# A decoder layer on one core: the first query block's products for the first half of the tokens moved between the two halves of keys and values, a tile of 32 extra rows, and five bridging products

## The chip, the core and the metric

The kernel runs on one core of a Trainium2 chip. The metric is the device time of one execution, in microseconds (us); the kernel before took 1930.22 to 1931.68 us in three runs, median 1931.51 us. A core has several engines, each with a queue of its own that it works through in order: TensorE (PE in the profile; its weight loads are the row PEld), VectorE (DVE), ScalarE (ACT), GpSimd (POOL) and SyncE (SP), which here only issues DMA transfers. An engine waits at the head of its queue until what its next instruction needs is there, and everything behind that instruction waits too. TensorE's clock is granted by the chip and shown in the profile as a share of full speed.

## The reference: what is computed

One step of a hybrid decoder layer for 512 prompt tokens, 16 learned meta tokens ahead of them and 8 single sample tokens, all in fp32, width 2048.

```python
hp = layer_norm(concat([meta, x_prompt]))      # 16 + 512 rows of 2048
hs = layer_norm(x_sample)                      # 8 rows
z = h @ w_in + b_in                            # columns: q 1024 | k 256 | v 256 | u 1024
q, k = partial_rope(q, pos), partial_rope(k, pos)
a = sink_attention(q, k, v, window=128)        # 16 heads of 64, 4 key/value heads, per-head sinks
p = pool_mixer(u)                              # trailing means over 2/4/8/16 positions, linear map, scale
h1 = layer_norm(ALPHA * h + concat([a, p]) @ w_o)
y = layer_norm(ALPHA * h1 + (silu(h1 @ w_gate) * (h1 @ w_up)) @ w_down)
```

The outputs are the new hidden rows of prompt and sample tokens, and the new windows of keys, values and pooling inputs.

## The kernel before

**Tokens and columns.** All activations are held transposed: features on the 128 partitions, tokens along the columns. There are 536 columns: 16 meta, 8 sample, 512 prompt. They are worked on in two halves: the first of 276 columns (0 to 275), the second of 260. Sixteen tiles of 128 features make up the width of 2048.

**A product in fp32.** Weights and activations are split into a high part, made by a cast to a shorter format, and the residual. Each product is three matmuls: high weight by high activation (L203), high by low (L204), low by high (L206). `split` casts a piece of weights, 128 x 512, on ScalarE (L187) and takes the residual on VectorE (L188). The two parts lie in a ring of places, `wh` and `wl`: seven places (WK) up to the end of keys and values, and after that a new ring of four (WA) laid over the room of the first. A cast into a place waits until the matmuls that read that place are done. The raw weights come by SyncE's DMA queue, 512 KB at a time, into a ring of five places (NRAW), and each such load waits for its place in that ring.

**The front.** The 536 token rows come in as four blocks of 128 rows (`xt`, each in four pieces of 512 columns) and one tile `xe` of the extra rows that do not fill a block: 32 rows around the end of the first half and 32 at the end of the second. `xe` is loaded first on SyncE; block 1 is loaded on ScalarE's own DMA queue, block 0 on SyncE's. Meanwhile TensorE multiplies constants 52 times (NWARM, L301); the result is not used. VectorE takes the statistics of the blocks (L310), ScalarE those of `xe` (L325 to L330). `normalisers` works out scale and shift, `x_norm` normalises (L341 on ScalarE; the extra rows on VectorE), `x_turn` transposes 128 x 128 pieces on TensorE into PSUM (L366), and `x_split` applies the gain and bias of the norm (L372 on VectorE, L375 on ScalarE), splits the result (cast L378 on ScalarE, residual L379 on VectorE) and writes it to memory on SyncE's queue.

**Keys and values** are the first products, the four column blocks 0 to 3 of `w_in`. They are made for the first half of the tokens, all sixteen feature tiles, and then for the second. In the loops, `kv_mm(h, k2)` is the step with the 24 matmuls for two feature tiles of half h, accumulating in four PSUM banks (`kv`), and the transposes, splits, and weight splits (`kv_weights`) for a later step stand between two such steps. Each key/value weight is loaded and split once per half. Between the last steps of the first half stand the first normalising and the first transposes of the second half's rows. After each half four instructions write the accumulators out with their bias, two on ScalarE (L477) and two on VectorE (L474).

**After that** come, in this order, query block 0 (`q_block(0)`: `in_block` makes the 96 products of both halves under each split piece of weights, four pieces for each of the two loads), pooling block 0, rotation of keys and their transposes, and then attention, further query and pooling blocks, the output projection, and the feed-forward part with its two norms.

**What sets the order.** The program is written as a list of steps, and a scheduler lays each engine's instructions into its queue by readiness and priority. In the front, `step(engines)` forces the order: on the engines named, every instruction of one step stands behind those of the step before. Inside a step, and after the front, the scheduler chooses. From query block 0 on, weight loads and splits have a raised priority (`prio[0] = WPRIO`). The places in the rings `wh`, `wl` and `raw` are handed out in the order of the program, one after the other.

Of the kernel before, what the change touches and what calls it, by code (L numbers as in the profile page):

```python
# [44 lines left out]
NWARM = 52  # L45
# [10 lines left out]
NB0 = C_P + P  # L56
SWAP = [i + 8 if i < 8 else i - 8 if i < 16 else i for i in range(32)]
# [10 lines left out]
def hybrid_step(ctx, tc, xin, w_in, w_o, w_g, w_u, w_d, w_pool, par_d, cst_d, ident_d, ln2gb, kct_d, vc_d, hist_d,  # L68
# [186 lines left out]
    with ExitStack() as sa:  # L255
# [32 lines left out]
        nc.sync.dma_start(xe[0:32], xin[256:288, :])  # L288
        nc.sync.dma_start(xe[32:64], xin[C_ALL - 32:C_ALL, :])
        nc.gpsimd.memset(xe[64:P], 0.0)  # L290
# [25 lines left out]
        def stats_e():  # L316

            t = pa.tile([P, 2, 2, 256], F32, tag="s", name="sq_e", bufs=2).rearrange("p a b c -> p (a b c)")[:64]
            ac = pa.tile([P, 2, 2], F32, name="ac")[:64]
            nm = pa.tile([P, 1], F32, name="nm_e")[:64]  # L320
            for i in range(2):
                for c in range(2):
                    x = xe[:64, c * 1024:(c + 1) * 1024]
                    if i == 0:
                        nc.scalar.activation(t, x, AF.Identity, accum_out=ac[:, i, c:c + 1])  # L325
                    else:
                        nc.scalar.activation(t, x, AF.Square, bias=nm, accum_out=ac[:, i, c:c + 1])
                nc.scalar.activation(t[:, 0:2], ac[:, i], AF.Identity, scale=1.0 / D, accum_out=mv[0][:64, 2, i:i + 1])
                if i == 0:
                    nc.scalar.activation(nm, mv[0][:64, 2, 0:1], AF.Copy, scale=-1.0)  # L330
# [20 lines left out]
        def x_norm(h, c):  # L351
            for i in range(2):
                norm[h](xt[2 * h + i][c], i, nc.scalar)
            if h == 0:
                norm[h](xe[:64, c * 512:(c + 1) * 512], 2, nc.vector)

        def x_turn(h, c):
            n = xw[h]
            for kk in range(4):
# [4 lines left out]
                for i in (0, 1, 2) if h == 0 else (2, 0, 1):  # L364
                    x, o = (xe[:, c * 512:(c + 1) * 512], 256 - 60 * h) if i == 2 else (xt[2 * h + i][c], i * P)
# [55 lines left out]

        three = (nc.tensor, nc.vector, nc.scalar)
# [13 lines left out]
        out = kv_banks(0)  # L436
        with step(*three):
            x_split(0, 0)
        with step(*three):
            kv_weights(0, range(4))  # L440
        for h in range(2):
            for g in range(4):
                n = h * 4 + g + 1
                with step(*three):
# [26 lines left out]
            with step(*three):  # L471
                for i in range(4):
                    if i % 2:
                        nc.vector.tensor_scalar(zkv[i][:, XH[h]], out[i], par[:, PBIAS + i:PBIAS + i + 1], None,  # L474
                                                op0=ALU.add)
                    else:
# [1045 lines left out]
```

## Time and profile before

| what | value |
|---|---|
| three runs | 1930.22, 1931.51, 1931.68 us; median 1931.51 |
| the profiled execution's own time (its span, first to last instruction) | 1931.1 us |
| mean granted clock of TensorE in it | 0.992 |
| instructions | 39334 |
| key/value matmuls (L203, L204, L206; 128 each in the records) | 32.4, 36.7 and 35.8 us busy |
| transposes of the front (L366; 64 and 32) | 9.8 and 6.3 us busy |
| normalising on ScalarE (L341, 16) | 12.1 us busy |
| HBM traffic | 265.22 MB read, 54.03 MB written |

The span is measured by the profiler inside the device; it lies 0.4 us under the median of the runs. A row of the page's groups gives source line, engine, operation, result and operands by the program's names (buffer numbers left out), shapes, count, busy time, mean length in ns, and then the time that the engine was idle just before these instructions, with what ended it ("<-"). Names: `rr` is the room of split weights and activations, `fr` and `mid_a` are rooms of fp32 tiles, `kv`, `xt`, `mm_q`, `mm_u` are PSUM tiles. A list of single instructions gives start and length in us from the span's start, engine, line and what it is, with the idle time ahead of it in brackets. In the table of windows each row is a stretch of the execution. A matmul with fp32 operands that are not split, such as the constant products and the transposes, can take two passes, and each pass is a record.

### The profile page before, as it was taken

Reading aid. Unit: us, or ns where it says so; the run is one execution under the profiler, and the core shown is the slowest. Engines: PE = TensorE matmul, PEld = TensorE weight load, DVE = VectorE, ACT = ScalarE, POOL = GpSimd, SP = SyncE. Lnnn points to the kernel's source line nnn. Section 1 sums busy time; section 2 is a strip of 40 time slices with the busy share of each in tenths; the row PEclk is TensorE's granted clock in tenths of the full one; section 3 lists DMA queues with packets and bytes.
Section 4 is the critical chain, followed back from the end, with each engine's and each line's share of the span. In section 5 each row is a group of like instructions: output and inputs, shape, how many; then the busy total and the mean of one; then the engine's idle time right before and its main releaser. Section 6 shows DMA issues by size and latency. Waiting matters only on the chain.

```text
span 1931.1 us, 39334 instructions
## 1 busy us (share of the span) xinstructions
PE 1894.4 (98%) x15533; PEld 1865.8 (97%) x15533; DVE 1539.9 (80%) x2734; ACT 944.1 (49%) x1808; POOL 2.7 (0%) x9
## 2 busy tenths in 40 slices
PE   9999999999999999999999999999999999999996
PEld 8999999999989999999999999999999999999996
DVE  6666667768777888888888888888877888888878
ACT  6644445545654544554455555555554444344341
POOL 0000000000000000000000000000000000000000
PEclk9999999999999999999999999999999999999998
DMA  8732222665744555454545445454469664645332
GB/s 276 233 101 66 71 78 75 211 202 193 250 150 164 160 160 172 142 162 158 175 139 178 141 138 165 146 167 145 164 212 356 214 221 162 223 163 202 94 99 89
DMA packets 145241, 319.28 MB, mean 165 GB/s; under 512 B 14288, under 2 KB 66232, under 8 KB 144952
## 3 DMA queue, kind: packets, MB, share of 16 engines
q1 hardware_dynamic: 144480, 315.71, 49.7%
q8 instruction: 122, 2.00, 0.4%
q10 hardware_dynamic: 576, 1.05, 0.2%
q14 instruction: 63, 0.52, 0.1%
HBM read 265.22 MB, written 54.03 MB: 165 GB/s over the span
## 4 chain that ended last, share of the span: by engine, by line
PE 92%; DVE 4%; ACT 2%; DMA 1%; issue 1%; SPq 0%; DVEq 0%; ACTq 0%
PE p_g L203 7%; PE p_g L204 7%; PE p_g L206 7%; PE p_u L203 7%; PE p_u L206 7%; PE p_u L204 7%; PE tri L203 7%; PE tri L206 7%; PE tri L204 7%; PE o L203 3%; PE o L206 3%; PE o L204 3%; PE p_u L996 2%; PE mm_u L203 2%; PE mm_u L206 2%; PE mm_u L204 2%
## 5 line engine op out<-in xcount | busy, mean ns | idle before, releaser
L187 ACT CAST rr<-fr 128x512 fp32r<-128x512 f32 (+1 forms) x1056 | 658.0, 643 | 776.6 <-DVE fr L196 224.0
L188 DVE TENSOR_TENSOR rr<-fr,rr 128x512 fp32r<-128x512 f32 (+1 forms) x1056 | 738.0, 717 | 264.5 <-ACT rr L187 253.2
L196 DVE TENSOR_TENSOR fr<-fr 128x1024 f32<-128x1024 f32 (+1 forms) x304 | 319.7, 1052 | 5.8 <-DMA fr<-in_w_g_dram 5.0
L203 PE MATMUL p_g<-rr 128*128 128x260 f32 x830 | 235.5, 285 | 7.4 <-ACT rr L187 7.1
L206 PE MATMUL p_g<-rr 128*128 128x260 f32 x830 | 230.6, 282 | 0.0
L204 PE MATMUL p_g<-rr 128*128 128x260 f32 x788 | 221.8, 282 | 0.0
L203 PE MATMUL p_u<-rr 128*128 128x260 f32 x770 | 217.5, 283 | 0.2 <-ACT rr L187 0.2
L206 PE MATMUL p_u<-rr 128*128 128x260 f32 x770 | 215.3, 282 | 0.0
L204 PE MATMUL p_u<-rr 128*128 128x260 f32 x748 | 210.6, 282 | 0.0
L206 PE MATMUL tri<-rr 128*128 128x260 f32 x696 | 196.8, 283 | 1.5 <-DVE rr L188 1.5
L203 PE MATMUL tri<-rr 128*128 128x260 f32 x696 | 197.0, 283 | 0.7 <-ACT rr L187 0.7
L204 PE MATMUL tri<-rr 128*128 128x260 f32 x696 | 196.7, 283 | 0.0
L203 PEld LDWEIGHTS p_g<-rr 128*128 128x128 f32 x830 | 156.2, 188 | 9.9 <-ACT rr L187 9.4
L206 PEld LDWEIGHTS p_g<-rr 128*128 128x128 f32 x830 | 155.2, 189 | 0.0
L204 PEld LDWEIGHTS p_g<-rr 128*128 128x128 f32 x788 | 148.1, 188 | 0.0
L203 PE MATMUL o<-rr 128*128 128x260 f32 x512 | 145.0, 284 | 0.3 <-ACT rr L187 0.3
L203 PEld LDWEIGHTS p_u<-rr 128*128 128x128 f32 x770 | 144.9, 188 | 0.3 <-ACT rr L187 0.3
L206 PEld LDWEIGHTS p_u<-rr 128*128 128x128 f32 x770 | 144.6, 189 | 0.0
L204 PE MATMUL o<-rr 128*128 128x260 f32 x512 | 144.1, 282 | 0.0
L206 PE MATMUL o<-rr 128*128 128x260 f32 x512 | 143.6, 282 | 0.2 <-DVE rr L188 0.2
L204 PEld LDWEIGHTS p_u<-rr 128*128 128x128 f32 x748 | 140.6, 188 | 0.0
L206 PEld LDWEIGHTS tri<-rr 128*128 128x128 f32 x696 | 131.3, 189 | 2.2 <-DVE rr L188 2.2
(320 smaller groups left out, 4570.0 us busy)
## 6 DMA issues: line engine op xcount, KB each, us to landing
fr<-in_w_u_dram SPq DMA_DIRECT2D x100, 512.0 KB
fr<-in_w_g_dram SPq DMA_DIRECT2D x90, 512.0 KB
fr<-in_w_d_dram SPq DMA_DIRECT2D x64, 640.0 KB
t_d<-fr SPq DMA_DIRECT2D x140, 260.0 KB
fr<-in_w_o_dram SPq DMA_DIRECT2D x64, 512.0 KB
fr<-in_w_in_dram SPq DMA_DIRECT2D x48, 512.0 KB
rr<-t_d SPq DMA_DIRECT2D x87, 260.0 KB
mid_b<-t_d SPq DMA_DIRECT2D x53, 260.0 KB
```

Of the source, the lines that this page charges most:

```text
L187: nc.scalar.copy(wh, s)
L188: last_lo[0] = (lo or nc.vector).tensor_sub(wl, s, wh.bitcast(F32)).ins
L196: i = op(*args).ins
L203: nc.tensor.matmul(o, wh, hi[j], start=first, stop=False, skip_group_check=onto)
L204: nc.tensor.matmul(o, wh, lo[j], start=False, stop=False, skip_group_check=onto)
L206: nc.tensor.matmul(o, wl, hi[j], start=False, stop=last, skip_group_check=onto)
L996: nc.tensor.matmul(bk, self.q(0, n - 1)[:, k * P:(k + 1) * P], z1[0][4 * (n - 1) + k // 2][:, k % 2, :], start=(k == 0), stop=(k == 7))
```

## The change

Four things are changed, all in the front and in query block 0.

1. **The tile of extra rows** has 32 rows (NE) where it had 64: 20 rows at the end of the first half (256 to 275), and the 12 last rows. Its loads, statistics, normalising and the offsets of its transposes follow.
2. **Warm-up and bridge.** NWARM is 50 where it was 52, and five further products of constants (NBRIDGE, L448) stand between the first transposes, `x_turn(0, 0)`, and the first `x_split` and key/value products. They write into a bank that the key/value products overwrite later.
3. **Query block 0, first half of the tokens.** Its 48 products (3 matmuls for each of 16 feature tiles) are made between the two halves of keys and values, in the generator `q0_half`: four chunks of twelve, each behind the split of its piece of weights. The order there is written out by hand for n = 4: chunk 1 in the step of `kv_mm(0, 6)`, chunk 2 in that of `kv_mm(0, 7)`, then three of the four groups of transposes of the second half's first rows, chunks 3 and 4, and the weight splits for the second half's first step. `load_kvw(1)` moves behind chunk 4.
4. **Query block 0, second half of the tokens** is made where the whole block was made before. Its weights are loaded and split there as before, so that they are now loaded and split twice. Its result `zq0` lies in the ring `q`, and the rotation is done in place.

All line numbers of the changed kernel are higher than before by 2 in the front and by more further on: L205, L206 and L208 are the three matmuls, L189 the cast and L190 the residual of a weight split, L279 a load of `xt`, L328 the first statistic of `xe`, L369 the transposes.

In the rows of order below, each row is one or more equal instructions in an engine's queue, with what they write and read. The first place is on TensorE, at the end of the first half of keys and values: `kv_0` are the first half's accumulators, `xt_0` the second half's transposes, `q_0` the moved query products. Before, and then in the change:

```order
L206 MATMUL kv_0_198<-rr 128x276
L203 MATMUL kv_0_198<-rr 128x276
L204 MATMUL kv_0_198<-rr 128x276
L206 MATMUL kv_0_198<-rr 128x276
L366 MATMUL xt_00_522<-fr,mid_a 128x128
L366 MATMUL xt_01_526<-fr,mid_a 128x128
```

```order
L205 MATMUL kv_0_197<-rr 128x276
L206 MATMUL kv_0_197<-rr 128x276
L208 MATMUL kv_0_197<-rr 128x276
L205 MATMUL q_0_526<-rr 128x260
L206 MATMUL q_0_526<-rr 128x260
L208 MATMUL q_0_526<-rr 128x260
```

The second half's transposes stood directly behind the key/value step `kv_mm(0, 6)`; now the first chunk of query products stands there, and the transposes come later.

The second place is on ScalarE, in the change, ahead of that first chunk: L239 is the square root of the second half's normaliser, L344 its normalising, L378 and L381 the last step of the first half's activation split, L189 x2 casts of query weights.

```order
L239 ACTIVATE mid_a<-mid_a 128x2
L344 ACTIVATE fr<-fr,mid_a 128x512 x2
L378 ACTIVATE fr<-xt_33_441,fr 128x276
L381 CAST rr<-fr 128x552
L189 CAST rr<-fr 128x512 x2
```

The casts of the query weights are new at this place, and they stand behind the normalising of the second half's rows.

The third place is on VectorE, at the end of the second half of keys and values and the start of the query products that follow. L474 and L427 write keys and values out, L395 and L398 rotate them, L188 and L190 are residuals of weight splits, L704 belongs to pooling. Before, and then in the change:

```order
L379 TENSOR_TENSOR rr<-fr,rr 128x520
L474 TENSOR_SCALAR mid_a<-kv_1_582,fr 128x260
L188 TENSOR_TENSOR rr<-fr,rr 128x512
L395 STREAM_SHUFFLE fr<-mid_a 128x536
L395 STREAM_SHUFFLE mid_a<-mid_a 128x536
```

```order
L190 TENSOR_TENSOR rr<-fr,rr 128x512
L427 TENSOR_SCALAR mid_a<-kv_1_617,fr 128x260
L398 STREAM_SHUFFLE mid_a<-mid_a 128x536
L190 TENSOR_TENSOR rr<-fr,rr 128x512 x2
L427 TENSOR_SCALAR mid_a<-kv_1_619,fr 128x260
L398 STREAM_SHUFFLE fr<-mid_a 128x536
L704 TENSOR_REDUCE mid_a<-fr 128x8
L190 TENSOR_TENSOR rr<-fr,rr 128x512
```

Before, the first residual of the query block (L188) stood behind the first write-out. In the change the residual that belongs to the first piece of the second query half is the last row shown; the three L190 rows above it belong to pieces two to four.

The diff, cut to its core:

```diff
-NWARM = 52
+NWARM = 50
+NBRIDGE = 5
...
+NE = 32
...
-        nc.sync.dma_start(xe[0:32], xin[256:288, :])
-        nc.sync.dma_start(xe[32:64], xin[C_ALL - 32:C_ALL, :])
-        nc.gpsimd.memset(xe[64:P], 0.0)
+        nc.sync.dma_start(xe[0:XN - 256], xin[256:XN, :])
+        nc.sync.dma_start(xe[XN - 256:NE], xin[C_ALL - NE + XN - 256:C_ALL, :])
+        for a, b in ((NE, 64), (64, P)):
+            nc.gpsimd.memset(xe[a:b], 0.0)
         load_x(1, nc.scalar)
         load_x(0)
...
-                    x = xe[:64, c * 1024:(c + 1) * 1024]
+                    x = xe[:NE, c * 1024:(c + 1) * 1024]
...
-        def x_turn(h, c):
+        def x_turn(h, c, kks=range(4)):
             n = xw[h]
-            for kk in range(4):
+            for kk in kks:
...
-                    x, o = (xe[:, c * 512:(c + 1) * 512], 256 - 60 * h) if i == 2 else (xt[2 * h + i][c], i * P)
+                    x, o = (xe[:, c * 512:(c + 1) * 512], 256 - (NE - 4) * h) if i == 2 else (xt[2 * h + i][c], i * P)
...
+        def zkv_out(h, i):
+            if i % 2:
+                nc.vector.tensor_scalar(zkv[i][:, XH[h]], out[i], par[:, PBIAS + i:PBIAS + i + 1], None, op0=ALU.add)
+            else:
+                nc.scalar.activation(zkv[i][:, XH[h]], out[i], AF.Identity, bias=par[:, PBIAS + i:PBIAS + i + 1])
...
         out = kv_banks(0)
+        with step(nc.tensor):
+            for j in range(NBRIDGE):
+                nc.tensor.matmul(out[3][:, 0:P], onesd, onesd, start=True, stop=True)
         with step(*three):
             x_split(0, 0)
         with step(*three):
             kv_weights(0, range(4))
+        zq0 = pa.tile([P, C_ALL], F32, tag="q", name="q0", bufs=3)
+
+        def q0_half(h):
+
+            cs, co = ((slice(META, XN), slice(META, XN)), (slice(0, xw[1]), XH[1]))[h]
+            o = (aux_tile([P, 512], "o", "q0_0", 1) if h == 0 else mm_tile("mm_q0_1"))[:, :cs.stop - cs.start]
+            for x in range(2):
+                raw = load_raw(w_in[4][:, x * 1024:(x + 1) * 1024], f"q0_{h}{x}")
+                for g in range(2):
+                    w = split(raw[:, g * 512:(g + 1) * 512], f"q0_{h}{x}{g}")
+                    for kk in range(4):
+                        k, sl = 8 * x + 4 * g + kk, slice(kk * P, (kk + 1) * P)
+                        products([o], w[0][:, sl], w[1][:, sl], [xhi[h][:, k, cs]], [xlo[h][:, k, cs]], k == 0, k == KT - 1)
+                    yield
+            nc.vector.tensor_scalar(zq0[:, co], o, par[:, PBIAS + 4:PBIAS + 5], 0.125, op0=ALU.add, op1=ALU.mult)
+            yield
+
         for h in range(2):
             for g in range(4):
                 n = h * 4 + g + 1
+                if n == 4:
+                    with step(*three):
+                        x_split(0, 7)
+                    for k2 in (6, 7):
+                        with step(*three):
+                            kv_mm(0, k2)
+                            if k2 == 6:
+                                q0 = q0_half(0)
+                                next(q0)
+                            else:
+                                next(q0)
+                                for i in range(4):
+                                    zkv_out(0, i)
+                    with step(*three):
+                        x_turn(1, 0, range(3))
+                    with step(*three):
+                        next(q0)
+                        x_split(1, 0)
+                    out = kv_banks(1)
+                    kvw.pop(0, None)
+                    with step(*three):
+                        next(q0)
+                        kv_weights(0, range(2))
+                    load_kvw(1)
+                    with step(*three):
+                        next(q0)
+                        x_turn(1, 0, [3])
+                        kv_weights(0, range(2, 4))
+                    continue
                 with step(*three):
                     x_split(h, 2 * g + 1)
...
-            with step(*three):
-                for i in range(4):
...
-                if h == 0:
-                    out = kv_banks(1)
+        with step(*three):
+            for i in range(4):
+                zkv_out(1, i)
...
         def q_block(t):
-            out = in_block(4 + t, f"q{t}", META)
-            z = zt_tile(f"zq{t}")
...
+            if t:
+                out = in_block(4 + t, f"q{t}", META)
+                z = zt_tile(f"zq{t}")
...
+            else:
+                for _ in q0_half(1):
+                    pass
+                z = q = zq0
             rope(z, q, f"q{t}", META)
```

25 lines of the change are left out of this document (10 added, 15 removed).

## The prediction

> **What bounds the kernel now.** I read the page's first parts, then the stretches of the clock, then who TensorE waited for, then the chain of waits and the order of time around each wait.
>
> ```profile
> span 1931.1 us, 39334 instructions
> PE 1894.4 (98%) x15533; PEld 1865.8 (97%) x15533; DVE 1539.9 (80%) x2734; ACT 944.1 (49%) x1808; POOL 2.7 (0%) x9
> PE 92%; DVE 4%; ACT 2%; DMA 1%; issue 1%; SPq 0%; DVEq 0%; ACTq 0%
> ```
>
> TensorE sets the time. It is busy for 98% of the span and makes 92% of the chain, so a microsecond won or lost on it in the first 110 us is carried to the end. The stretches below give, for each, its length and the busy time of PE, PEld, DVE, ACT and POOL, then the granted clock, the DMA share and GB/s.
>
> ```profile
> 0.00:14.40 14.40, 13.27 (x104) 13.08 (x104) 6.24 (x15) 7.27 (x16) 2.46 (x8) 1.00 0.87 275
> 14.40:17.80 3.40, 1.76 (x12) 1.31 (x12) 1.51 (x5) 1.96 (x3) 0.00 (x0) 0.97 1.05 390
> 17.80:21.20 3.40, 2.21 (x10) 2.00 (x9) 2.54 (x5) 3.37 (x8) 0.00 (x0) 0.50 1.05 385
> 21.20:24.60 3.40, 3.40 (x18) 3.40 (x16) 2.95 (x6) 3.40 (x6) 0.00 (x0) 0.53 1.09 356
> 24.60:48.50 23.90, 23.43 (x185) 22.62 (x183) 19.62 (x38) 13.80 (x25) 0.00 (x0) 1.00 0.75 233
> 48.50:51.90 3.40, 2.09 (x11) 1.31 (x12) 1.07 (x5) 2.94 (x5) 0.00 (x0) 0.97 0.16 60
> 51.90:55.30 3.40, 3.40 (x16) 3.40 (x17) 2.74 (x5) 2.31 (x6) 0.00 (x0) 0.52 0.38 123
> 55.30:82.50 27.20, 27.20 (x232) 27.16 (x231) 17.82 (x32) 19.99 (x38) 0.00 (x0) 1.00 0.80 231
> 82.50:110.00 27.50, 27.17 (x226) 26.65 (x227) 17.84 (x38) 10.32 (x23) 0.00 (x0) 1.00 0.64 233
> ```
>
> Two things are lost in the front: holes in TensorE's work, and the half clock behind each. A stretch of 3.4 us in which it was busy for 1.76 us (52%) is followed by 6.8 us near 0.50; one with 2.09 us (61%) by 3.4 us at 0.52; after 2.21 us (65%) the half clock stays. Each such stretch, filled, costs half its length: 1.7 us. From 55.3 to 110 only 0.33 us is idle.
>
> **The change, part by part.** All sums are against the profiled span of 1931.1 us; the median of the runs, 1931.51, lies 0.4 above it, and I add the sum to the median.
>
> *Smaller tile of extra rows, 50 warm-up products.* Fewer bytes come first, but the fourth piece of the second token block, whose issue stood ahead of the statistics on ScalarE's queue, now stands behind the first statistic, which waits for the extra rows.
>
> ```profile
> 7.18 1.06 ACT L325 ACTIVATE mid_a<-mid_a 64x1024 f32<-64x1024 f32 x1 [4.01 <-DMA mid_a<-in_xin_dram]
> 9.04 3.22 DVE L310 BATCH_NORM_STATS2 mid_a<-fr 128x6 f32<-128x512 f32 x5 [0.82 <-DMA fr<-in_xin_dram]
> ```
>
> At 390 GB/s 256 KB are 0.7 us, at 275 1.0 us: the gain, at most. The moved piece, two places later, lands some 1.4 us later than in turn, and VectorE needs it sixth of eight; the loss is at most that. I take 0, with −1.0 and +1.3 as ends. ScalarE's casts get no cheaper by fewer rows, since a row of a tile is a partition.
>
> *Five bridging products.* They stand between the first transposes and the first key/value products.
>
> ```profile
> 0.99 13.27 PE L301 MATMUL wb<-fr 128*128 128x128 f32 x104 [0.99 <-POOL fr L143]
> 15.89 0.55 PE L366 MATMUL xt<-fr 128*128 128x128 f32 x3 [1.63 <-ACT fr L341]
> 19.20 0.60 PE L203 MATMUL kv<-rr 128*128 128x276 f32 x1 [1.19 <-ACT rr L187]
> ```
>
> Each product is two passes (104 for 52), 128 ns on average. Two fewer warm-ups widen the 1.63 us hole by 0.5 us, so the stretch ahead stays low and the half clock still comes. Ten passes at half clock are 10 x 0.26 = 2.6 us against a hole of 1.2: they hold the first products up by some 1.0 us. But the stretch is then full, and the clock rises one stretch (3.4 us) sooner: −1.7. Net −0.8. If the clock never falls, the 5.4 us of half clock from 19.2 to 24.6 give −2.7; if it rises no sooner, the delay is left, +1.0.
>
> *Query products into the hole between the halves.* The first instructions behind the last but one key/value step were transposes; now they are twelve query products, and the transposes have gone behind these (TensorE's rows of order, shown with the change). On ScalarE, by its rows there, the query cast (L189) stands behind the very work that made the hole. Before, it went so (TensorE's rows, then the chain of waits with start, length and what):
>
> ```profile
> 47.86 0.38 PE L366 MATMUL xt<-fr,mid_a 128*128 128x128 f32 x2
> 49.52 0.30 PE L366 MATMUL xt<-fr,mid_a 128*128 128x128 f32 x1 [1.28 <-DVE fr L372]
> ...
> 28.00 0.63 ACT rr L187
> ...
> 48.93 0.49 ACT fr L341
> ...
> 50.95 0.66 ACT rr L378
> 51.65 1.25 PE kv L203 x4
> ```
>
> From 28.00, where ScalarE was let go by a TensorE product, to 51.65 the chain runs on ScalarE and VectorE alone. So the hole ends when that chain ends, whatever is queued. Before, TensorE did twelve transposes in it. After, nothing can run; the twelve come behind it (36 in the rows below, 4.9 us summed but started 0.11 us apart: 1.3 us for twelve), and the hole is longer by one cast (0.62, started 0.53 apart) and a wait of 0.4 for its residual on VectorE. That is +2.2 us, the opposite of filling.
>
> ```profile
> L187 ACT CAST rr<-fr 128x512 fp32r<-128x512 f32 x49 | 28.5, 618 | 18.6 <-PE mm_q L204 9.5 <-PE mm_u L204 5.9 <-PE kv L204 2.8
> L188 DVE TENSOR_TENSOR rr<-fr,rr 128x512 fp32r<-128x512 f32 x49 | 32.0, 686 | 7.0 <-ACT rr L187 6.9
> L366 PE MATMUL xt<-fr 128*128 128x128 f32 x24 | 3.1, 272 | 0.0
> L366 PE MATMUL xt<-fr,mid_a 128*128 128x128 f32 x12 | 1.8, 276 | 0.0
> ```
>
> Ends: 0, if the sooner clock moves the chain further than TensorE; +3.9, if the longer hole costs a second slow stretch. The 96 products themselves move at no price. Their weights are loaded and split twice: two more loads of 512 KB on SyncE's queue between the writes of the normalised stream, four more casts (2.1 us) and four residuals (2.4 us). They lie under the second half's products, where ScalarE has 7.2 us and VectorE 9.4 us free of 27.2, and DMA a fifth; without that cover they would cost 2.4.
>
> *Start of the second query half.* This is the new wait. The weight ring of seven is closed after the halves, and its room becomes the ring of four. Thirty-two splits went through it, now thirty-six: the last split then sits in place 0, where the next ring has its first cast. So the first query piece is cast last of its four. VectorE's rows of order there are shown with the change too. The residual that TensorE's third query product needs was second; it is now the last row there, behind three other pieces' residuals, and the first of them starts only when TensorE is within its last eight products and two transposes. Before, the same kinds of row took:
>
> ```profile
> 83.01 0.49 DVE L474 TENSOR_SCALAR mid_a<-kv,fr 128x260 f32<-128x260 f32 x1 [3.20 <-PE kv L206]
> 83.42 0.68 DVE L188 TENSOR_TENSOR rr<-fr,rr 128x512 fp32r<-128x512 f32 x1
> 84.02 0.78 DVE L395 STREAM_SHUFFLE fr<-mid_a 128x536 f32<-128x536 f32 x1
> 85.36 0.48 DVE L474 TENSOR_SCALAR mid_a<-kv,fr 128x260 f32<-128x260 f32 x1
> 85.75 1.28 DVE L188 TENSOR_TENSOR rr<-fr,rr 128x512 fp32r<-128x512 f32 x2
> 86.95 0.16 DVE L647 TENSOR_REDUCE mid_a<-fr 128x8 f32<-128x8 f32 x1
> 83.53 0.27 PE L507 MATMUL tqv<-fr,mid_a 128*16 128x128 f32 x1
> 83.66 0.36 PE L203 MATMUL mm_q<-rr 128*128 128x260 f32 x1
> ```
>
> By their starts: 0.60 + 0.41 + 0.67 + 1.20 + 0.39 + 0.67 + 0.08 + 0.68 = 4.7 us. It begins 0.9 us before TensorE's queue of keys and values is done, so the residual is there 3.8 us after; two products fill 0.2, and the 0.33 us that the stretch up to 110 lost before goes. Net +3.4 (3.0 to 3.8). A hole of 3.6 us is longer than any that dropped the clock before: one slow stretch costs 1.7, two 3.4; I take 2.5.
>
> The Trainium skill, on its page "TensorE: Matmul & The Clock Gate" (section "Part 1: The HAM clock gate"), says the clock falls after at least one idle window of about 3.4 us, free-running. Here it fell after a stretch that was 61% busy, so I go by the rows; by the page this term would mostly vanish, and the sum be 2.5 lower.
>
> Sum: 0 − 0.8 + 2.2 + 3.4 + 2.5 = +7.3, and 1931.5 + 7.3 = **1938.8 us**.
>
> **The rivals.**
> *The holes fill (faster).* If the query casts were ready before 47.86 and the first residual of the second half in time, the hole's 1.28 + 0.16 us idle, most of its other gaps (3.4 − 2.09 in all = 1.3) and its slow stretch (1.7) would go, with −2.7 at the bridge: about −5.7, 1925.8. It decides from the point where ScalarE's L189 x2 ends ahead of the key/value step. Against it stand both rows of order; for it only that the chain ahead could shorten if TensorE is no longer slow at 19 to 24.
> *Given back.* The bridge keeps the clock up (−2.7), the chain then ends sooner and the hole costs 0, the second half's wait stays with one slow stretch: −2.7 + 3.4 + 1.7 = +2.4, 1933.9. For it: that chain starts at a TensorE release.
> *No slow stretch after the new wait.* A clock that needs a wholly idle stretch leaves 7.3 − 2.5 = +4.8, 1936.3. Against it: the 61%.
> *All dear.* The late piece (+1.3), a second slow stretch in the hole (+1.7) and after the new wait (+0.9): +11.2, 1942.7.
>
> **How the numbers follow.** Forecast 0.60 (its own range 1936.5 to 1942), all dear 0.10, no slow stretch 0.08, given back 0.14, holes fill 0.08. A measurement of this kernel tells about 0.2% (3.9 us) from no change. Slower than that: 0.60 + 0.10 + 0.08 = 0.78; within: 0.14; faster: 0.08. The range leaves out the fast rival and the top of the dear one: 1933 to 1943.
>
> **What would show it.** TensorE's waits: a row for L208 of the second query half on VectorE's L190 with over 3 us; a row for q L205 on ScalarE's L189 of 2.5 us or more ahead of the second half's transposes; clock rows near 0.5 behind both; the clock back at 1.0 near 21, not 24.6. Wrong would be: no wait at the second query half, or the first second-half key/value product less than 4 us later than before although 5.8 us of query products (48 at 0.12) now precede it.

## The result, and the profile after

The changed kernel takes **1942.76 us** (median of four runs, 1941.99 to 1943.99) against 1931.6 beside it: a ratio of 1.0058, 95% interval 1.0046 to 1.0070, so 11.2 us slower (8.9 to 13.5). The forecast was 1938.8, +7.3, with a range of 1933 to 1943. The profiled execution is 10.0 us longer than the one before, and the sums below are made on it. (A span lies some 1.9 us under the time of the same execution: 1941.1 for 1942.93 here, 1930.9 for 1932.94 in a later one of the kernel before. So the execution before that was profiled, with 1931.1, was about 1.4 us above its median, which is what lies between 10.0 and 11.2.) The head of its page:

```profile
span 1941.1 us, 39354 instructions
PE 1898.0 (98%) x15539; PEld 1868.6 (96%) x15539; DVE 1542.9 (79%) x2738; ACT 946.5 (49%) x1812; POOL 4.5 (0%) x10
PE 92%; DVE 3%; ACT 2%; DMA 1%; issue 1%; SPq 0%; DVEq 0%; ACTq 0%
```

Nothing in it tells where 10 us went; shares over the whole span do not show 0.5%. The stretches of the first 110 us do (columns as before: length, busy time of PE, PEld, DVE, ACT, POOL, granted clock, DMA share, GB/s):

```profile
14.40:17.80 3.40, 1.92 (x14) 1.38 (x14) 1.45 (x8) 1.52 (x2) 0.00 (x0) 1.00 1.05 385
17.80:21.20 3.40, 3.19 (x24) 2.82 (x23) 2.45 (x5) 3.23 (x7) 0.00 (x0) 1.00 1.05 388
...
47.50:51.00 3.50, 0.05 (x1) 0.00 (x0) 1.26 (x6) 2.51 (x4) 0.00 (x0) 0.99 0.24 90
51.00:54.40 3.40, 2.66 (x10) 2.36 (x11) 1.94 (x3) 1.16 (x3) 0.00 (x0) 0.50 0.27 89
54.40:57.80 3.40, 3.40 (x17) 3.40 (x16) 0.00 (x0) 0.00 (x0) 0.00 (x0) 0.50 0.43 149
...
95.30:98.70 3.40, 0.24 (x3) 0.12 (x2) 3.05 (x9) 0.00 (x0) 0.00 (x0) 1.00 0.84 257
98.70:102.10 3.40, 3.40 (x16) 3.40 (x17) 3.40 (x6) 0.62 (x1) 0.00 (x0) 0.51 1.09 407
```

The half clock behind the first transposes (17.8 to 24.6 before) is gone. In its place there are two stretches in which TensorE does next to nothing (47.5 to 51.0 and 95.3 to 98.7), with three stretches of half clock behind them, two and one. TensorE's waits from 14 to 110 us name what it waited for:

```profile
PE q L205 <- ACT rr L189: 4.1, 1, 4.1
PE mm_q L208 <- DVE rr L190: 3.2, 1, 3.2
...
PE mm_q L205 <- ACT rr L189: 0.5, 1, 0.5
```

The first row is the first moved query product, waiting for its weight's cast; the second is the third product of the second query half, waiting for its residual; the last is that half's first cast. To see where TensorE gains and loses, compare when it starts the same work. Before:

```profile
24.72 0.38 PE L366 MATMUL xt<-fr 128*128 128x128 f32 x2
47.73 0.29 PE L206 MATMUL kv<-rr 128*128 128x276 f32 x1
60.44 0.49 PE L203 MATMUL kv<-rr 128*128 128x260 f32 x2
67.51 0.37 PE L203 MATMUL kv<-rr 128*128 128x260 f32 x1
96.28 0.36 PE L203 MATMUL mm_u<-rr 128*128 128x276 f32 x1 [0.33 <-DVE fr L528]
109.18 0.40 PE L547 MATMUL sc<-mid_a 64*128 64x152 f32 x2
```

After:

```profile
23.26 0.49 PE L369 MATMUL xt<-fr 128*128 128x128 f32 x3
47.26 0.29 PE L208 MATMUL kv<-rr 128*128 128x276 f32 x1
51.70 0.59 PE L205 MATMUL q<-rr 128*128 128x260 f32 x1 [4.14 <-ACT rr L189]
69.86 0.49 PE L205 MATMUL kv<-rr 128*128 128x260 f32 x2
78.03 0.37 PE L205 MATMUL kv<-rr 128*128 128x260 f32 x1
105.97 0.29 PE L205 MATMUL mm_u<-rr 128*128 128x276 f32 x1
119.03 0.53 PE L604 MATMUL sc<-mid_a 64*128 64x152 f32 x4
```

The end of the first key/value step, where the second group of transposes starts, comes at 23.26 us; before it was at 24.72, so the change is 1.46 us ahead. The last product of the step ahead of the hole starts at 47.26, against 47.73: 0.47 ahead. The second half's second step (60.44, then 69.86) is 9.42 late. Since 48 query products stand ahead of it that did not before (twelve take 1.45 us at full clock, so 5.8 us), 3.6 of it is loss, and with the 0.47 the stretch from the hole to this step has cost 4.1. From this step to the fourth (67.51, 78.03) another 1.1 is lost. At the first pooling product (96.28, 105.97) all query products are done in both, and the whole difference, 9.7, is loss: 9.7 − (10.52 − 5.8) = 5.0 belongs to the second query half. At the first attention scores it is 9.85, at the end 10.0.

Not all of the 4.1 is lost in the hole itself. The fourth chunk of query products waits once more, for the cast and then for the residual of its weights:

```profile
63.34 0.39 PE L205 MATMUL q<-rr 128*128 128x260 f32 x1
64.16 0.39 PE L208 MATMUL q<-rr 128*128 128x260 f32 x1 [0.31 <-DVE rr L190]
```

The third and fourth chunk take 3.9 us (61.59 to 65.45) where 2.9 would do. ScalarE's cast for the fourth (62.67) stands behind the split of the second half's first activations (62.14).

### The profile page after: what moved, and what is told of

The parts are those of the page before. It is cut to its first block, busy times and chain, and to the rows that moved or that the text cites. A ratio compares the mean times of both kernels' runs of the same rounds, so it can differ in the third digit from the quotient of the medians.

```text
span 1941.1 us, 39354 instructions
## 1 busy us (share of the span) xinstructions
PE 1898.0 (98%) x15539; PEld 1868.6 (96%) x15539; DVE 1542.9 (79%) x2738; ACT 946.5 (49%) x1812; POOL 4.5 (0%) x10
## 4 chain that ended last, share of the span: by engine, by line
PE 92%; DVE 3%; ACT 2%; DMA 1%; issue 1%; SPq 0%; DVEq 0%; ACTq 0%
PE p_g L205 8%; PE p_g L206 7%; PE p_g L208 7%; PE p_u L205 7%; PE p_u L208 7%; PE p_u L206 7%; PE tri L205 7%; PE tri L208 7%; PE tri L206 6%; PE o L205 3%; PE o L208 3%; PE o L206 3%; PE p_u L1053 2%; PE mm_u L205 2%; PE mm_u L208 2%; PE mm_u L206 2%
## 5 line engine op out<-in xcount | busy, mean ns | idle before, releaser
L189 ACT CAST rr<-fr 128x512 fp32r<-128x512 f32 (+1 forms) x1060 | 660.4, 643 | 777.0 <-DVE fr L198 218.0
L190 DVE TENSOR_TENSOR rr<-fr,rr 128x512 fp32r<-128x512 f32 (+1 forms) x1060 | 739.7, 715 | 266.6 <-ACT rr L189 253.3
L205 PE MATMUL p_g<-rr 128*128 128x260 f32 x830 | 235.6, 285 | 7.4 <-ACT rr L189 7.1
L208 PE MATMUL p_g<-rr 128*128 128x260 f32 x830 | 230.7, 282 | 0.0
L206 PE MATMUL p_g<-rr 128*128 128x260 f32 x788 | 221.9, 282 | 0.0
L205 PE MATMUL p_u<-rr 128*128 128x260 f32 x770 | 217.5, 283 | 0.0
L208 PE MATMUL p_u<-rr 128*128 128x260 f32 x770 | 215.4, 282 | 0.0
L206 PE MATMUL p_u<-rr 128*128 128x260 f32 x748 | 210.8, 282 | 0.0
L208 PE MATMUL tri<-rr 128*128 128x260 f32 x696 | 196.9, 283 | 2.1 <-DVE rr L190 2.1
L205 PE MATMUL tri<-rr 128*128 128x260 f32 x696 | 197.1, 283 | 0.7 <-ACT rr L189 0.7
L206 PE MATMUL tri<-rr 128*128 128x260 f32 x696 | 196.9, 283 | 0.0
L205 PEld LDWEIGHTS p_g<-rr 128*128 128x128 f32 x830 | 156.3, 188 | 9.9 <-ACT rr L189 9.4
L208 PEld LDWEIGHTS p_g<-rr 128*128 128x128 f32 x830 | 155.3, 189 | 0.0
L206 PEld LDWEIGHTS p_g<-rr 128*128 128x128 f32 x788 | 148.2, 188 | 0.0
L205 PE MATMUL o<-rr 128*128 128x260 f32 x512 | 145.2, 284 | 0.3 <-ACT rr L189 0.3
L205 PEld LDWEIGHTS p_u<-rr 128*128 128x128 f32 x770 | 145.0, 188 | 0.0
L208 PEld LDWEIGHTS p_u<-rr 128*128 128x128 f32 x770 | 144.7, 189 | 0.0
L206 PE MATMUL o<-rr 128*128 128x260 f32 x512 | 144.1, 282 | 0.0
L208 PE MATMUL o<-rr 128*128 128x260 f32 x512 | 143.8, 282 | 0.2 <-DVE rr L190 0.2
L206 PEld LDWEIGHTS p_u<-rr 128*128 128x128 f32 x748 | 140.6, 188 | 0.0
L208 PEld LDWEIGHTS tri<-rr 128*128 128x128 f32 x696 | 131.3, 189 | 2.9 <-DVE rr L190 2.9
```

The costliest lines, as they stand in the source:

```text
L189: nc.scalar.copy(wh, s)
L190: last_lo[0] = (lo or nc.vector).tensor_sub(wl, s, wh.bitcast(F32)).ins
L205: nc.tensor.matmul(o, wh, hi[j], start=first, stop=False, skip_group_check=onto)
L206: nc.tensor.matmul(o, wh, lo[j], start=False, stop=False, skip_group_check=onto)
L208: nc.tensor.matmul(o, wl, hi[j], start=False, stop=last, skip_group_check=onto)
```

## The experiments

Ratios are to the kernel before, run beside each; the last column is the ratio's distance from 1, times 1931.6 us.

| kernel | ratio, 95% interval | against before |
|---|---|---|
| the whole change | 1.0058 (1.0046 to 1.0070) | +11.2 |
| move alone | 1.0055 (1.0042 to 1.0068) | +10.6 |
| bridge alone | 0.9997 (0.9988 to 1.0006) | −0.6 |
| extra rows alone | 1.0001 (0.9992 to 1.0010) | +0.2 |
| change, ring place skipped | 1.0033 (1.0020 to 1.0045) | +6.4 |
| change, statistics later | 1.0036 (1.0022 to 1.0050) | +7.0 |
| change, both | 1.0008 (1.0000 to 1.0017) | +1.5 |
| both, statistics later still | 0.9995 (0.9986 to 1.0003) | −1.0 |
| change, one load left out | 1.0046 (1.0034 to 1.0058) | +8.9 |
| change, holes filled with constants | 1.0042 (1.0030 to 1.0055) | +8.1 |
| mended, load order | 0.9988 (0.9979 to 0.9997) | −2.3 |
| mended, load order and raw order | 0.9990 (0.9981 to 0.9999) | −1.9 |
| bridge, extra rows, load order; no move | 0.9992 (0.9983 to 1.0001) | −1.5 |

**The parts.** The move alone:

```diff
-NWARM = 50
-NBRIDGE = 5
+NWARM = 52
+NBRIDGE = 0
...
-NE = 32
+NE = 64
```

(the loads of the extra rows are those of before).

> The changed kernel with 52 warm-up products, no bridge and the tile of 64 extra rows, so the kernel before with only the query products moved. My theory: the move alone carries the whole loss, and more than the whole change's +11.2 us, since the bridge's gain goes: 1942.5 to 1945.5, with the holes of over 4 us at the first query product and over 3 us at the second query half. Rival 'the smaller tile and the bridge cost': under 1940.

Median 1942.2, a little under the expected range. It carries the whole loss, with the same two waits, of 4.1 and 2.7 us; bridge and smaller tile make no difference in the times. The bridge alone, in the kernel before:

```diff
-NWARM = 52
+NWARM = 50
+NBRIDGE = 5
...
         out = kv_banks(0)
+        with step(nc.tensor):
+            for j in range(NBRIDGE):
+                nc.tensor.matmul(out[3][:, 0:P], onesd, onesd, start=True, stop=True)
```

> The kernel before with only the 50 warm-up and five bridging products. My theory: the clock stays at 1.00 behind the bridge as in the changed kernel, TensorE gains 1.5 us by 24 us, but the chain on VectorE and ScalarE ahead of the hole between the halves gives back a part: -0.5 to -1.5 us, about 1930.6. Rival 'all of the half-clock stretch is kept': -2.7 us, 1928.9. Rival 'the bridge costs': 1932.5 or more.

Median 1931.12. In its profile the clock is 1.00 throughout the first 290 us, the first key/value step ends at 23.09 us (before 24.72), and `kv_mm(0, 7)` starts at 51.00 (before 51.65): 1.6 us won, 0.65 left behind the hole, and in the times nothing that can be told from none (0.9988 to 1.0006). Its chain of waits between the two, start, length and what (in part):

```profile
35.58 0.68 DVE rr L189
36.27 2.38 DVE mid_a L311 x4
...
45.12 1.21 DVE mid_a L311 x2
...
48.27 0.49 ACT fr L342
...
50.29 0.66 ACT rr L379
```

There is no row of TensorE in it from 24 to 51 us (it comes out of a transfer of input rows that ends at 24.84): VectorE's statistics of the second half (L311) and what follows them set when the hole ends, and a TensorE that is earlier only waits longer. The extra rows alone:

```diff
+NE = 32
...
-        nc.sync.dma_start(xe[0:32], xin[256:288, :])
-        nc.sync.dma_start(xe[32:64], xin[C_ALL - 32:C_ALL, :])
+        nc.sync.dma_start(xe[0:XN - 256], xin[256:XN, :])
+        nc.sync.dma_start(xe[XN - 256:NE], xin[C_ALL - NE + XN - 256:C_ALL, :])
```

> The kernel before with only the tile of 32 extra rows. My theory: the extra rows come 1.0 us sooner, but the fourth piece of the second token block, now issued behind their first statistic, leaves VectorE waiting some 2 us, and the first transposes start 0.4 to 0.6 us later than at 15.89 us; the time is within noise of before, 1931.7 to 1933. Rival 'fewer bytes first are a gain': transposes at 15 us, about 1930.7.

Median 1932.47; the first transposes start at 16.27 (before 15.89). VectorE's rows show the late piece:

```profile
8.31 1.29 DVE L312 BATCH_NORM_STATS2 mid_a<-fr 128x6 f32<-128x512 f32 x2 [0.19 <-DMA fr<-in_xin_dram]
11.33 1.29 DVE L312 BATCH_NORM_STATS2 mid_a<-fr 128x6 f32<-128x512 f32 x2 [1.74 <-DMA fr<-in_xin_dram]
```

It waits 1.74 us for the piece whose load had gone behind the first statistic on ScalarE. What the smaller tile brought sooner, that load gave back. In this execution the clock stayed at 1.00 in the front without a bridge. With the bridge it did so in all eleven profiles; without it, it fell there in the kernel before and with the move alone. That speaks for the bridge, but it does not tell what five products are worth.

**The wait at the second query half.** The prediction put it down to the place in the weight ring. One place of the new ring is skipped:

```diff
         sp[:] = [Pool(rr), WA]
+        for t in ("wh", "wl"):
+            sp[0].tile([P, 512], F32R, tag=t, bufs=WA)
```

> The changed kernel with one place of the new weight ring skipped, so that the second query half's first cast goes into a place that is free early, and its residual stands ahead of the keys' and values' write-out on VectorE. Nothing else is changed. My theory (the place in the ring makes the wait): the wait of 3.16 us and the half clock behind it (1.7) go, -4 to -5 us, about 1938.0, no row of over 0.5 us at the second query half. Rival 'VectorE is simply late there, or held by the transfer it waits for (0.35 us)': at most -1, about 1942.

Median 1938.03. VectorE in the changed kernel, at the end of the second half of keys and values:

```profile
93.41 0.69 DVE L190 TENSOR_TENSOR rr<-fr,rr 128x512 fp32r<-128x512 f32 x1 [2.44 <-DMA fr<-in_w_in_dram]
94.02 0.48 DVE L427 TENSOR_SCALAR mid_a<-kv,fr 128x260 f32<-128x260 f32 x1
...
94.43 0.76 DVE L398 STREAM_SHUFFLE mid_a<-mid_a 128x536 f32<-128x536 f32 x1
95.07 1.28 DVE L190 TENSOR_TENSOR rr<-fr,rr 128x512 fp32r<-128x512 f32 x2
96.26 0.48 DVE L427 TENSOR_SCALAR mid_a<-kv,fr 128x260 f32<-128x260 f32 x1
...
97.77 0.17 DVE L704 TENSOR_REDUCE mid_a<-fr 128x8 f32<-128x8 f32 x1 [0.35 <-DMA fr<-in_hist_dram]
97.85 0.68 DVE L190 TENSOR_TENSOR rr<-fr,rr 128x512 fp32r<-128x512 f32 x1
```

It is the sequence of the prediction, 93.41 to 98.53 = 5.1 us where 4.7 was summed; the rest is 0.35 us for a transfer. With the skipped place VectorE does the same work in the same order, but by the order of the ring the residual at the head is now the first piece's, and TensorE's waits behind 50 us are:

```profile
PE q L205 <- ACT rr L189: 4.1, 1, 4.1
PE kv L205 <- ACT rr L381: 0.5, 1, 0.5
PE q L208 <- DVE rr L190: 0.3, 1, 0.3
```

The wait of the second query half is gone, as is the half clock behind it; VectorE is as busy as it was. So not its load made the wait, but which residual stood last.

**The hole between the halves.** The last statistics, the normaliser and the first normalising of the second half go behind the first query chunk's split:

```diff
-                if n < 4:
+                if n < 3:
                     with step(*three):
                         for _ in range((1, 2, 1)[g]):
                             next(later.pop(0))
-                        if n == 3:
-                            norm[1] = normalisers(1)
-                            x_norm(1, 0)
...
                                 q0 = q0_half(0)
                                 next(q0)
+                                next(later.pop(0))
+                                norm[1] = normalisers(1)
+                                x_norm(1, 0)
```

> The changed kernel with the last statistics, the normaliser and the first normalising of the second half moved from ahead of the first half's last activation split to behind the first chunk's weight split. My theory (the hole lasts as long as this chain stands ahead of the cast): the 4.14 us of idle time and the 3.0 us of half clock at the hole go, and 0 to 3 us of it come back at the second half's transposes, -4 to -7 us, about 1937.5. Rival 'the hole only moves to the transposes': 1942 to 1943, with a wait of 3 to 4 us on L344.

Median 1938.15. TensorE's waits from 14 us on:

```profile
PE mm_q L208 <- DVE rr L190: 2.7, 1, 2.7
PE xt L369 <- ACT fr L344: 2.1, 2, 1.9
PE q L208 <- DVE rr L190: 1.8, 3, 1.3
```

The wait of 4.1 us for ScalarE is gone, and it has not moved to the second half's transposes: the 1.9 us on L344 are at the first half's first transposes, at 16.56 us. What is left, 1.3 us, is for VectorE: inside the step the scheduler set the last two statistics ahead of the chunk's residual. Both edits together:

> Both edits together in the changed kernel: one place of the new weight ring skipped, and the last statistics, normaliser and first normalising of the second half behind the first chunk's weight split. My theory: the two stalls are independent, so the gains add (-4.7 and -4.6 in the medians): about 1933.5, 1932 to 1935. Rival 'they share a cause' (VectorE late from the hole on): 1936 or more.

Median 1933.0, 9.7 us below the change, where the two alone gave 4.8 and 4.2: they add, within the intervals. Then the statistics in the step of `kv_mm(0, 7)`, and the write-out of keys and values in a step behind it:

```diff
                             else:
+                                next(later.pop(0))
+                                norm[1] = normalisers(1)
+                                x_norm(1, 0)
                                 next(q0)
-                                for i in range(4):
-                                    zkv_out(0, i)
+                    with step(*three):
+                        for i in range(4):
+                            zkv_out(0, i)
```

> As the kernel with both edits, but the statistics and the normaliser stand in the step of kv_mm(0, 7), behind the first chunk's residual, and the write-out of keys and values in a step after it. My theory: the 1.34 us that the first query chunk's third product still waits for VectorE go too: 1932.3, 1930.5 to 1934. Rival: later chunks' residuals are pushed behind and take it back: no better than the kernel with both edits.

Median 1930.51, lower than expected by 1.8 and no longer slower than before. The 1.3 us are gone from the first chunk, but the rival was partly right: the third chunk's third product now waits 0.8 us for its residual, and a key/value product 1.1 us for the cast L381. From the last step ahead of the moved products to the first scores it takes 59.5 us (47.64 to 107.16) against 60.3 (47.90 to 108.18), so the traces show 0.8 of the 2.5 by which the medians differ, and the intervals of the two kernels overlap. This is the mended kernel of the experiments below.

**The late load.** The 1.1 us lost between the starts of the second half's second and fourth steps had no term in the prediction. ScalarE in the changed kernel:

```profile
70.86 0.62 ACT L189 CAST rr<-fr 128x512 fp32r<-128x512 f32 x1 [1.73 <-DMA fr<-in_w_in_dram]
```

The second of the extra loads is left out:

```diff
-                raw = load_raw(w_in[4][:, x * 1024:(x + 1) * 1024], f"q0_{h}{x}")
+                if x == 0 or h:
+                    raw = load_raw(w_in[4][:, x * 1024:(x + 1) * 1024], f"q0_{h}{x}")
```

> The changed kernel without the second of the two extra loads of query weights for the first half: the first tile is split again in its place, so the query's values for the first half are wrong in their second half of feature tiles. Splits, products and order stay. My theory: with one tile fewer in the ring of five, the weight load for the second half's second step comes earlier, ScalarE's wait of 1.73 us for it and TensorE's 1.1 us behind it go: -1.1 us, 1941.7. Rival 'VectorE and ScalarE are full of the extra splits': the 1.1 us stay, 1942.8.

Median 1940.51. ScalarE no longer waits there, and the stretch from the second step's start to the next transposes takes 5.83 us (69.72 to 75.55) where it took 6.94 (69.86 to 76.80); TensorE's 0.46 us of wait in it are gone too. All extra casts and residuals were still there, so the loads were the cause: two more tiles go through the ring of five, and the next key/value loads have to wait for a place (in the change SyncE's loads L287 wait for residuals L190, the last readers of a place, for 8.3 us in five waits). The median fell by 2.3 us, twice the 1.1: in the profiled execution the half clock behind the second wait stayed away as well, although that wait was still there, so the times alone do not measure the load. The same was then cured without leaving anything out, in the mended kernel (with the load order that is described at the end of this section), by loading both query tiles ahead of the second half's first weights:

```diff
-                        if n < 7:
+                        if n == 3:
+                            q0raw = [load_raw(w_in[4][:, x * 1024:(x + 1) * 1024], f"q0_0{x}") for x in range(2)]
+                        elif n < 7:
                             load_kvw((n + 1) % 4)
...
+                    load_kvw(0)
                     with step(*three):
                         x_split(0, 7)
```

(and `load_kvw(1)` ahead of `x_turn(1, 0, range(3))`).

> As the kernel with the load order, and both extra loads of query weights stand ahead of the second half's first key/value loads in the ring of five, with the second step's loads right behind the second query chunk. My theory: ScalarE's wait of 2.4 us for a load at 65 us and TensorE's 1.1 us at 68 us go: -1.0 us, about 1928.5. Rival: another load is late in its place, no gain, 1929.5.

Median 1929.89; the same stretch took 7.04 us (62.75 to 69.79) in the mended kernel with the load order alone, and takes 5.83 (62.78 to 68.61). In the medians the difference of 0.4 cannot be told from none.

**The clock.** To part it from the waits, products of constants are put into the two holes:

```diff
+NHOT = (15, 10)
...
                     w = split(raw[:, g * 512:(g + 1) * 512], f"q0_{h}{x}{g}")
+                    for j in range(NHOT[h] if x + g == 0 else 0):
+                        nc.tensor.matmul(o[:, 0:P], onesd, onesd, start=True, stop=True)
```

> The changed kernel with 15 products of constants ahead of the first query chunk (15 x 0.256 = 3.8 us in a hole of 4.14) and 10 ahead of the second query half (2.6 us in a wait of 0.5 + 3.16). They hide no work; the waits stay as long. My theory: no stretch falls under some 57% busy, so the clock stays at 1.00, and the half clock's 3.0 us at the hole and 1.7 us behind the second wait go: -4 to -5 us, about 1938.2. Rival 'the clock falls whatever TensorE does there': 1942.8 or, with products in the way, more.

Median 1939.94 (1937.61 to 1943.93), 3.1 us by the ratio, somewhat less than expected. In its profile:

```profile
48.00:51.40 3.40, 3.40 (x32) 3.40 (x31) 1.41 (x7) 2.23 (x4) 0.00 (x0) 1.00 0.32 104
51.40:54.80 3.40, 2.27 (x17) 1.87 (x16) 1.94 (x3) 1.45 (x3) 0.00 (x0) 1.00 0.23 78
...
96.00:99.40 3.40, 2.99 (x25) 2.99 (x26) 3.40 (x7) 0.80 (x2) 0.00 (x0) 1.00 0.83 299
```

The clock stays at 1.00. From the last product of the step ahead of the hole to the first scores it takes 67.3 us (47.95 to 115.27) against 71.8 (47.26 to 119.03), 4.5 us less with no useful work hidden. So much the three stretches of half clock cost. The kernel before had one of its own there, of 1.7 us, so of the loss of 9.1 up to the second step and in the second query half about 3 us are clock and the rest is waiting. This one execution is only 0.5 us shorter in the whole than the change's: it lost 1.8 us again by a further stretch of half clock near 350 us, and 1.4 between 1760 and 1830 us.

**The load order, and the kernel without the move.** In the mended kernel all four loads of the second block go ahead of the statistics on ScalarE's queue:

```diff
-        load_x(1, nc.scalar)
+        with step(nc.scalar):
+            load_x(1, nc.scalar)
```

> The kernel with the skipped place and the statistics in the step of kv_mm(0, 7), and in it all four loads of the second token block ahead of the statistics on ScalarE's queue. My theory: VectorE's wait of 2.1 us for the fourth piece goes, the first transposes start near 15.0 us in place of 16.5, and the time falls by 0.5 to 1.5 us, about 1929.5. Rival 'the transfers are at their limit and the piece lands no sooner': 1930.5.

Median 1930.3 against 1930.51: no difference in the medians. The first transposes start at 16.02 us, not at 15.0. VectorE's rows tell why:

```profile
7.17 0.69 DVE L314 BATCH_NORM_STATS2 mid_a<-fr 128x6 f32<-128x512 f32 x1 [1.23 <-DMA fr<-in_xin_dram]
8.62 1.39 DVE L314 BATCH_NORM_STATS2 mid_a<-fr 128x6 f32<-128x512 f32 x2 [0.76 <-DMA fr<-in_xin_dram]
10.50 1.88 DVE L314 BATCH_NORM_STATS2 mid_a<-fr 128x6 f32<-128x512 f32 x3 [0.48 <-DMA fr<-in_xin_dram]
```

The wait of 2.1 us for the fourth piece is gone, and the earlier pieces are waited for instead, 2.5 us in sum: they come at the rate of the transfers, whichever is first (from 6 to 12 us the DMA engines' share is 0.99). The rival was right here: the order is worth 0.5 us at the first transposes, and nothing that the times show. Last, everything but the move:

> The kernel before with the bridge, the tile of 32 extra rows and the loads ahead of the statistics, but without moving query products. It tells what the move is worth once its stalls are mended: this against the kernel with the raw order. My theory: about 1930.3; the mended move is better by 1 to 2 us, what the hole between the halves cost before (1.4 us idle, and a slow stretch in some executions). Rival 'the move gains nothing even when mended': this one is as fast or faster, 1929 or less.

Median 1931.25. The mended move with the raw order is 1.4 us below it in the medians and 0.4 by the ratios, with intervals that overlap (0.9981 to 0.9999 and 0.9983 to 1.0001): that the move gains anything when mended is not shown. In the traces it is ahead early on. The first scores start at 104.90 us, here at 107.40; one group of transposes (`tpv`) stands behind them there and ahead of them here, and at the next query products, with the same work done, it is 2.1 us (107.07 and 109.16). Of these 1.7 are the stretch of half clock that only the kernel without the move had, at 50.1 us. At 442 us 0.2 us are left, and in the whole the profiled execution with the move is the longer one (1928.4 against 1927.5).

## Why the prediction was right or wrong

The direction, both waits and their places were right; the size came out 2.7 us too small on the profiled execution (7.3 against 10.0) and 3.9 on the medians. By its steps:

| step | forecast | profiled execution |
|---|---|---|
| extra rows, warm-up and bridge, up to the hole | −0.8 | −0.5 |
| hole between the halves, up to the second step | +2.2 | +4.1 |
| loads, casts and residuals of the weights split twice | 0 | +1.1 |
| second query half: wait 3.4, clock 2.5 | +5.9 | +5.0 |
| behind it | 0 | +0.3 |

*Extra rows.* Zero was right for the time, with both halves of the argument as told: rows 1.0 us sooner (7.18, then 6.15), and the moved piece late. The transposes start 0.5 us later.

*Bridge.* The clock did not rise a stretch sooner, it never fell, which the text had as the end of −2.7. The gain was 1.46 us at 23 us. What failed is the carrying: the sum let a gain of TensorE run on to the hole, though the prediction's own rows of the chain show that only ScalarE and VectorE are in it from 28 us on. The bridge alone shows the same loss of gain, 1.6 to 0.65. The rival "given back" rested on the reverse, a chain that ends sooner when TensorE does. The chain passed on 0.48 of the 1.46 us (its last activation cast starts at 50.47, and at 50.95 before), and the query cast behind it used that up: 51.70, and 51.65 before.

*Hole.* The mechanism was right: the query cast stood behind the chain that made the hole, and taking the chain away took the wait away. The 1.8 us for twelve transposes and one cast came out as worked out: from the product ahead of the hole to the one behind it 4.44 us (47.26 to 51.70), where it had been 3.92 with 1.3 us of transposes in it. The term that was mis-sized is the clock, some 1.3 us in place of none. It was given one slow stretch, as before, with a second only in the dear end of +3.9; there were two. The stretches of the clock have fixed bounds, one of them at 50.95 us here. TensorE began at 51.70, so it was busy for 77% of the next stretch, and that did not raise the clock; it needed the one after. With the skipped ring place the bound fell at 51.23, just ahead of its 51.30:

```profile
47.80:51.20 3.40, 0.00 (x0) 0.00 (x0) 1.11 (x4) 3.11 (x6) 0.00 (x0) 1.00 0.15 54
51.20:54.60 3.40, 3.25 (x13) 2.95 (x14) 1.49 (x3) 0.57 (x2) 0.00 (x0) 0.50 0.34 106
54.60:58.00 3.40, 3.40 (x29) 3.40 (x28) 0.69 (x2) 1.06 (x3) 0.00 (x0) 0.99 0.32 109
```

There one stretch was enough, behind a hole of the same length (4.1 us), and by the same reckoning the hole cost 2.9. So the price of a hole in clock depends on where a bound lies. The other 0.9 us had no term: the chunks behind the hole were given no wait for their splits, and the fourth chunk's came late, behind an activation split on ScalarE. The mended kernels still lose it: the two chunks take 4.1 us with the raw order (54.25 to 58.35), where the third waits for its residual. No run removes this wait.

*Weights loaded twice.* The step that failed is the cover: free time of ScalarE and VectorE and a fifth of the DMA engines were named, and these were free. The place in the ring of raw tiles was not looked at. It is a resource like an engine, and no row of busy time shows its use; only the waits of later loads do.

*Second query half.* The idle time was 3.16 + 0.50 us where 3.6 was worked out, and its cause is shown by the skipped place. One slow stretch followed, not one and a half.

The Trainium skill's page "TensorE: Matmul & The Clock Gate" (section "Part 1: The HAM clock gate") lets the clock fall after an idle window and calls the windows free-running. At both new holes the stretch ahead of the half clock was all but idle (0.05 us busy, and 0.24), so rule and row agree there, and the 2.5 us that the prediction said would mostly vanish by the page did not: they were 1.7. In the kernel with the smaller tile alone the clock fell with TensorE busy for 1.98 us of 3.4 and no idle time over 1.3 us, against the rule:

```profile
47.00:50.40 3.40, 1.98 (x13) 1.20 (x13) 1.46 (x7) 2.15 (x5) 0.00 (x0) 1.00 0.36 119
50.40:53.80 3.40, 3.40 (x15) 3.17 (x16) 2.82 (x5) 2.58 (x5) 0.00 (x0) 0.50 0.24 83
```

## What to carry to other kernels

Work that is to fill a hole must have everything it needs ahead of the chain that makes the hole, on every engine that prepares it: here twelve ready transposes were exchanged for products whose cast stood last in that very chain. Count the shared places too: four more pieces through a ring of weights changed which cast of a later step had to wait, and two more raw tiles delayed a load of the next half, while every engine had time to spare. A gain on the busiest engine is worth what is left of it at the next wait for another one.

## What the runs showed of the hardware

In these traces the clock turned only at bounds a multiple of 3.413 us apart. By the clock records it fell at 17.59 and 51.72 us in the kernel before (ten such lengths apart) and at 50.95 and 98.73 in the changed one (fourteen); the bounds lie at other places from the span's start in every profiled execution. Whether a hole costs no slow stretch, one or two depends on where it lies against the bounds: the same 4.1 us hole cost two in the change and one with the skipped place. This is probably one reason why single executions of a kernel differ by 2 to 7 us (1933.98 to 1941.30 with the skipped place); no kernel here has two profiles that would show it.

How much work keeps the clock up stayed open. Taken between the bounds, over the first 110 us of all profiles: after stretches of which TensorE was busy for 37% or less it always fell, after 61% or more never; between 48% and 58% it did both. Rising took more than that: a stretch of which TensorE was busy for 77% (50.95 to 54.36 in the change) left it at half, one of 96% (51.23 to 54.64 with the skipped place) raised it.
